# First feed-forward block of a hybrid decoder: four covered tiles in place of six, a longer run of zero products at the opening, and another order for the first halved unit of each block

## The chip, the core and the metric

One core of one Trainium2 chip runs the whole program. Its engines work side by side, each through its own queue in order: TensorE (PE; its weight loads are listed apart as PEld), VectorE (DVE), ScalarE (ACT), GpSimd (POOL) and SyncE (SP), which here only starts transfers. The metric is the device time of one execution in microseconds.

## What is computed

A decoder trunk of two layers on x, 512 tokens of width 1024, in float32. In a layer:

```
x = x + 1/2 * SwiGLU_a(RMSNorm(x))        # first FFN, width 2816
h = RMSNorm(x) @ W_mix_in                 # three token mixers share one projection
y = concat[shortconv | HGRN2 | FoX]
x = x + y @ W_mix_out
x = x + 1/2 * SwiGLU_b(RMSNorm(x))        # second FFN
swiglu(h, w_in, w_out) = (silu(gate) * up) @ w_out,   gate, up = split(h @ w_in)
rms_norm(x, gain) = x * rsqrt(mean(x*x) + 1e-6) * gain
```

The change touches the four FFNs (two of each layer), above all the first one, with which the program opens.

## The kernel before

**Number format.** Each float32 operand is cut into a high part, which ScalarE casts, and a low part, which VectorE gets as operand minus high part. A product is then three matmuls (`mm3`, L387): high by high, high by low, low by high.

**The two ways to compute an FFN.** D_FF is 22 tiles of 128 features, taken in pairs. The first `covered` tiles are *covered*: plain products over all 512 tokens, of x that has its gain but is not yet normalised (`cover`, L627). A pair of tiles takes four steps of two of the eight tiles of x; a step is 24 matmuls of 512 columns, and a pair 96. The results lie in four PSUM banks until 1/rms is known; "clear t" then multiplies the two banks of tile t by it, "silu t" and "values t" finish the tile. The purpose of the covered tiles is that TensorE has work while the norm is computed and the operands of the rest are built.

The rest is *halved* (`halved`, L781): a matrix product by two-by-two blocks with seven products instead of eight, P1 to P7, for a unit of two tiles. Each product is 24 matmuls of 256 columns, so a unit has 168. A product needs two things. Its *operand* on the x side is built once for each FFN: quarters of the normalised x ("x a b", `normalise` L746, four VectorE instructions), sums of them ("+ a b c d", L678), and then the two parts (`operand` L759: ScalarE L774 or L779, VectorE L775 or L779). P1 takes quarter 00, P5 00+01, P6 that plus 11, P4 that plus 10; P2 takes 10, P7 01+11, P3 11. Its *weights* are blocks 0 to 3 of w_in, or sums of them: P1 block 0, P2 block 1, P5 2+3, P6 the sum S of P5's block and block 0, P7 block 0 plus 2, P3 block 1 plus S, P4 block 3. Some sums are VectorE instructions ("sum", L829), some are transfers of GpSimd that add to what lies in the tile ("add" L816; "adds" L859, which adds S to block 1). `prepare` (L831) cuts the weights of a product in two parts (ScalarE L841, VectorE L843), three products ahead (`LEAD`), into one of three buffers `hl`; the buffer comes free when TensorE has finished the product three before.

**The order.** `ENTRY[covered]` is written by hand: at step n of the covered tiles (n = 4 to 2*covered-1), at the three first preparations, and after each product from then on, `deal(n)` (L663) issues the work listed under n. `follow` chains these instructions of ScalarE, VectorE, GpSimd and the transfers, so that each engine takes them just in the program's order. The first FFN has covered = 6 and its first 4 steps are the opening; the other three have covered = 4. `ORDER_IN` is the order of the seven products of a unit. `plan(covered)` (L80) works out a sequence of all products and when loads, sums and adds are issued; for the first unit it issues "adds" ahead of the first product, behind the preparation of P1, P2 and P6. After its product, P1 is copied out of its bank (g1, L933), P2 subtracted from it (L936) and given to silu; P6 is copied out (g2, L940) and P5 too (u2, L943); P7 then goes on summing in the bank that P6 was copied from.

The four banks of a unit's first three new sums are those of the first covered pair: P1 needs tile 0 cleared, and the third new sum needs tile 1 cleared.

**The opening.** `open_x` (L1715) and `idle` (L1743) start the program: two products of zeros (tile `none`) on TensorE, the gain, the first 128 columns of x transposed, one more product of zeros, and then the first matmuls (L445), high part of the weights first. Each product of zeros takes its bank anew.

Of the kernel before, what the change touches and what calls it, by code (L numbers as in the profile page):

```python
# [8 lines left out]
F32 = mybir.dt.float32  # L9
F32R = mybir.dt.float32r  # L10
# [15 lines left out]
P = 128  # L26
T = 512
# [8 lines left out]

ORDER_IN = ("P1", "P2", "P6", "P5", "P7", "P3", "P4")
ORDER_OUT = ("P2", "P1", "P5", "P6", "P7", "P3", "P4")
LEAD = 3
# [11 lines left out]
    },  # L51
# [5 lines left out]
    },  # L57
# [22 lines left out]
def plan(covered):  # L80
# [6 lines left out]
    into = lambda c: [  # L87
        ("I", f, p) for f in range(max(covered, c[0]), c[0] + c[1], 2) for p in ORDER_IN
    ]
# [25 lines left out]
    for u in dict.fromkeys((k, w) for k, w, _ in seq):  # L115
# [5 lines left out]
        if kind == "I":  # L121
            end = {0: "P7", 1: "P3", 2: "P5", 3: "P4"}
            m = split["P6"] - 1
            if w == covered:

                when(-1, 5, "add", u, 0, 2)
                when(-1, 6, "adds", u)
                continue
            else:
                begin[2] = m - 1 - AHEAD_SUM - AHEAD_LOAD  # L130
                begin[3] = split["P7"] - 2 - AHEAD_LOAD
                when(m - 1 - AHEAD_SUM, 5, "add", u, 2, 3)
                between(m - 1, m, "total", u, "S2")
                when(max(m, split["P2"]), 6, "adds", u)
                between(max(m, split["P1"]) + 1, split["P7"] - 1, "total", u, "S3")
        else:
            end = {0: "P7", 1: "P2", 2: "P3", 3: "P4"}
            begin[2] = split["P5"] - AHEAD_SUM - AHEAD_LOAD
            when(split["P5"] - AHEAD_SUM, 5, "add", u, 2, 3)
            if w[0]:  # L140
                when(split["P5"] + 1, 5, "add", u, 2, 0)
            else:
                between(split["P5"] + 1, split["P5"] + 2, "total", u, "S2")
            when(split["P5"] + 3, 5, "add", u, 0, 2)
            when(split["P6"] + 1, 5, "add", u, 2, 1)
# [38 lines left out]
class Trunk:  # L184
# [8 lines left out]
    def __init__(self, ctx, tc):  # L193
        self.tc = tc
        self.nc = tc.nc
        nc = self.nc
        self.const = ctx.enter_context(tc.tile_pool(name="const", bufs=1))
        self.res = ctx.enter_context(tc.tile_pool(name="res", bufs=1))
# [5 lines left out]
            tc.tile_pool(name="dram", bufs=1, space=bass.MemoryType.DRAM)  # L204
        )
        self.ident = self.const.tile([P, P], F32, tag="ident", name="ident")
        make_identity(nc, self.ident)
        self.ones_mean = self.const.tile([P, P], F32, tag="ones_mean", name="ones_mean")
        nc.vector.memset(self.ones_mean, 1.0 / D)
        self.epsc = self.const.tile([P, 1], F32, tag="epsc", name="epsc")  # L210
        nc.vector.memset(self.epsc, EPS)
        self.xT = self.res.tile([P, KD, T], F32, tag="xT", name="xT")

        self.none = self.res.tile([P, T], F32R, tag="inv", name="none")
        nc.vector.memset(self.none.bitcast(F32), 0.0)

        self.xh, self.xl = [None] * KD, [None] * KD
        self.uid = 0
        self.ntog = 0
        self.tab, self.tab_users = None, []  # L220
        self.chain = {}

# [184 lines left out]
    def stream_steps(  # L407
# [17 lines left out]
        while k < nk:  # L425
# [36 lines left out]
            for n, ((acc, cols, toks, *more), j) in enumerate(order):  # L462
                if pre is not None and n == len(order) // 2:
                    pre(k, True)
                if fine and n == len(order) // 2:
                    yield
# [160 lines left out]
    def cover(self, fp, w_in, w_out, covered, mean, begin):  # L627
# [35 lines left out]
        def deal(n):  # L663
            if n == mean and begin is None:
                squares()
            for what in filter(None, ENTRY[covered].get(n, "").split(", ")):
                name, *at = what.split()
# [25 lines left out]
        for f in range(0, covered, 2):  # L693
            banks = self.next4()

            def parts(k, kk, f=f):
# [8 lines left out]
                (lambda *a: self.open_x(x, gain, fp, *a)) if opening else None,  # L705
                None if opening else (lambda k, f=f: deal(2 * f + k // 2)), begin is None or f > 2,

# [73 lines left out]
    def halved(self, fp, w_in, w_out, covered, deal):  # L781
# [107 lines left out]
        u = seq[0][:2]  # L889
        for q in (2, 0, 3, 1):  # L890
            raw[u, q] = t = fp.tile(
                [P, 4, 2 * P], F32, tag=("mh", "ml")[q % 2], name=self.n("w"), bufs=2
            )
            S(nc.sync.dma_start(t, src(u, q)))
# [820 lines left out]
    def open_x(self, x, gain, fp, k, loaded=False):  # L1715
# [6 lines left out]
        if not loaded:  # L1722
            if k == 0:
                self.idle(2)
                self.begin_norm(gain, fp)
# [3 lines left out]
                self.load_open(0)  # L1729
                self.idle(1)  # L1730
                self.xb[1] = self.load_x(x, 1, fp, True)
# [11 lines left out]
    def idle(self, n):  # L1743

        for _ in range(n):
            b = self.bank("po")
            self.follow("p", self.nc.tensor.matmul(b, self.none[:, :P], self.none, start=True, stop=True))
# [27 lines left out]
def trunk_kernel(  # L1775
# [47 lines left out]
```

## Time and profile before

| | us |
|---|---|
| median of 3 runs | 1831.99 (1830.6 to 1832.21) |
| the profiled execution, its own time | 1832.37 |
| its span, first to last instruction | 1830.6 |
| TensorE busy (matmuls) | 1821.0 |
| VectorE busy | 1445.3 |
| ScalarE busy | 1001.7 |

The profile's times are microseconds from the start of the span. In a timeline a row has the start, the duration, engine, line of the kernel, operation and tiles, and in brackets the idle time before it with what ended it. A matmul's duration holds its pipeline, so for a run of matmuls it is the distance of their starts that counts. In the chain of waits the durations are already such distances.

### The profile page before, as it was taken

Reading aid. Unit: us, or ns where it says so; the run is one execution under the profiler, and the core shown is the slowest. Engines: PE = TensorE matmul, PEld = TensorE weight load, DVE = VectorE, ACT = ScalarE, POOL = GpSimd, SP = SyncE. Lnnn points to the kernel's source line nnn. Section 1 sums busy time; section 2 is a strip of 40 time slices with the busy share of each in tenths; the row PEclk is TensorE's granted clock in tenths of the full one; section 3 lists DMA queues with packets and bytes.
Section 4 is the critical chain, followed back from the end, with each engine's and each line's share of the span. In section 5 each row is a group of like instructions: output and inputs, shape, how many; then the busy total and the mean of one; then the engine's idle time right before and its main releaser. Section 6 shows DMA issues by size and latency. Waiting matters only on the chain.

```text
span 1830.6 us, 31999 instructions
## 1 busy us (share of the span) xinstructions
PE 1821.0 (99%) x12934; PEld 1674.7 (91%) x12934; DVE 1445.3 (79%) x1965; ACT 1001.7 (55%) x1414; POOL 185.1 (10%) x190
## 2 busy tenths in 40 slices
PE   9999999999999999999999999999999999999999
PEld 7899999888888899999889999998888888999997
DVE  8889786679677888879678887976777778888883
ACT  5455554465666465555445555555656655555552
POOL 0011120100000101112001111201000001020210
PEclk9999999999999999999999999999999999999999
DMA  7668783242543767868276787823425438677762
GB/s 214 177 134 189 177 180 94 68 124 68 127 110 96 216 136 168 193 165 174 81 202 140 174 183 190 163 69 84 114 74 127 119 98 217 161 152 196 154 135 92
DMA packets 249908, 262.38 MB, mean 143 GB/s; under 512 B 19816, under 2 KB 228464, under 8 KB 249760
## 3 DMA queue, kind: packets, MB, share of 16 engines
q1 hardware_dynamic: 193904, 192.15, 35.7%
q0 software_dynamic: 55840, 68.19, 23.4%
q8 instruction: 101, 1.65, 0.4%
q14 instruction: 47, 0.39, 0.1%
q10 hardware_dynamic: 16, 0.00, 0.0%
HBM read 226.15 MB, written 2.17 MB: 125 GB/s over the span
## 4 chain that ended last, share of the span: by engine, by line
PE 96%; ACT 1%; DVE 1%; DMA 1%; issue 0%; SPq 0%; DVEq 0%; ACTq 0%
PE mm L392 14%; PE mm L399 14%; PE mm L398 14%; PE sc L392 6%; PE sc L399 6%; PE sc L398 6%; PE pt L392 6%; PE pt L399 6%; PE pt L398 6%; PE po L392 4%; PE po L399 4%; PE po L398 4%; PE sc L1600 1%; PE po L1655 1%; PE sc L1414 1%; PE pt L1637 1%
## 5 line engine op out<-in xcount | busy, mean ns | idle before, releaser
L841 ACT CAST hl<-w 128x1024 fp32r<-128x1024 f32 x322 | 337.7, 1050 | 347.6 <-PE mm L399 81.9
L843 DVE TENSOR_TENSOR hl<-w,hl 128x1024 fp32r<-128x1024 f32 x322 | 392.5, 1220 | 87.2 <-ACT hl L841 87.0
L379 DVE TENSOR_TENSOR hl<-st,hl 128x1024 fp32r<-128x1024 f32 (+3 forms) x152 | 160.0, 1053 | 120.4 <-ACT hl L378 119.7
L378 ACT CAST hl<-st 128x1024 fp32r<-128x1024 f32 (+3 forms) x152 | 138.6, 912 | 176.3 <-PE po L399 81.5
L392 PE MATMUL mm<-xc,hl 128*128 128x256 f32 (+1 forms) x730 | 201.4, 276 | 0.3 <-ACT g L940 0.3
L399 PE MATMUL mm<-xc,hl 128*128 128x256 f32 x728 | 201.4, 277 | 0.0
L398 PE MATMUL mm<-xc,hl 128*128 128x256 f32 x728 | 201.2, 276 | 0.0
L392 PE MATMUL sc<-xc,hl 128*128 128x256 f32 (+1 forms) x530 | 146.4, 277 | 0.6 <-ACT g L940 0.6
L399 PE MATMUL sc<-xc,hl 128*128 128x256 f32 x528 | 146.1, 277 | 0.0
L398 PE MATMUL sc<-xc,hl 128*128 128x256 f32 x528 | 146.0, 277 | 0.0
L392 PEld LDWEIGHTS mm<-xc,hl 128*128 128x128 f32 x730 | 137.0, 188 | 0.8 <-ACT g L940 0.5
L398 PEld LDWEIGHTS mm<-xc,hl 128*128 128x128 f32 x728 | 136.8, 188 | 0.0
L399 PEld LDWEIGHTS mm<-xc,hl 128*128 128x128 f32 x728 | 136.6, 188 | 0.1
L392 PE MATMUL pt<-xc,hl 128*128 128x256 f32 (+1 forms) x482 | 132.7, 276 | 0.0
L398 PE MATMUL pt<-xc,hl 128*128 128x256 f32 x480 | 132.7, 276 | 0.0
L399 PE MATMUL pt<-xc,hl 128*128 128x256 f32 x480 | 132.6, 276 | 0.0
L392 PE MATMUL mm<-x,hl 128*128 128x512 f32 x272 | 108.8, 400 | 0.0
L399 PE MATMUL mm<-x,hl 128*128 128x512 f32 x272 | 106.1, 390 | 0.0
L398 PE MATMUL mm<-x,hl 128*128 128x512 f32 x272 | 105.9, 389 | 0.0
L392 PEld LDWEIGHTS sc<-xc,hl 128*128 128x128 f32 x530 | 99.5, 188 | 1.5 <-ACT g L940 1.0
L399 PEld LDWEIGHTS sc<-xc,hl 128*128 128x128 f32 x528 | 99.2, 188 | 0.1
L398 PEld LDWEIGHTS sc<-xc,hl 128*128 128x128 f32 x528 | 99.1, 188 | 0.0
(487 smaller groups left out, 5470.6 us busy)
## 6 DMA issues: line engine op xcount, KB each, us to landing
w<-in_ffn_w_in_dram SPq DMA_DIRECT2D x140, 512.0 KB
w<-in_ffn_w_out_dram SPq DMA_DIRECT2D x64, 512.0 KB
w<-in_ffn_w_out_dram POOLq DMA_DIRECT2D x56, 512.0 KB, 9.0
st<-in_w_mix_in_dram SPq DMA_DIRECT2D x80, 256.0 KB
w<-in_ffn_w_in_dram POOLq DMA_DIRECT2D x39, 512.0 KB, 8.1
st<-in_ffn_w_in_dram SPq DMA_DIRECT2D x70, 256.0 KB
w<-S POOLq DMA_DIRECT2D x35, 512.0 KB, 4.7
st<-in_ffn_w_out_dram SPq DMA_DIRECT2D x24, 512.0 KB
```

The source lines that it names most:

```text
L378: a = nc.scalar.copy(hi, src[:, c : c + w])
L379: b = nc.vector.tensor_sub(lo, src[:, c : c + w], hi)
L392: i = nc.tensor.matmul(acc[:, c], ah, bh[:, c], start=first and c.start == 0, stop=False, skip_group_check=True,)
L398: nc.tensor.matmul(acc, ah, bl, start=False, stop=False, skip_group_check=True)
L399: i = nc.tensor.matmul(acc, al, bh, start=False, stop=last, skip_group_check=True)
L841: A(nc.scalar.copy(hi, src))
L843: return lambda: V(nc.vector.tensor_sub(lo, src, hi))
L1414: nc.tensor.matmul(s2[:, :, t], e[:, i * P : (i + 1) * P], e2[:, :, t], start=True, stop=True)
L1600: mm = lambda *a, **k: E(nc.tensor.matmul(*a, skip_group_check=True, **k))
L1637: E(nc.tensor.transpose(tb[:, k * P : (k + 1) * P], to[u][:, j * P : (j + 1) * P], self.ident))
L1655: E(nc.tensor.matmul(self.ob[:, o], half[2][:, j, h].rearrange("p a d -> p (a d)"), part[:, at[0] : at[-1] + 1, :].rearrange("p b t -> p ( ...
```

## The change

The first FFN takes four covered tiles, and its `ENTRY` is a new one of its own, "opening". The other FFNs keep `ENTRY[4]`. All four take a new order for the seven products of their first unit, load its blocks in another order, and issue the first unit's "adds" behind the preparation of P2, which is now the fourth (so behind the first product, no longer ahead of it). The covered steps can be dealt work at their middle too (key 4.5). The tile of zeros is set first of all; four and three products of zeros are issued, for two and one, each group into one bank that is taken once.

```
 ORDER_IN = ("P1", "P2", "P6", "P5", "P7", "P3", "P4")
+ORDER_FIRST = ("P1", "P5", "P6", "P2", "P7", "P3", "P4")
...
-    6: {
-        7: "norm, x 0 0", 8: "x 1 0, clear 0, clear 1", 9: "silu 0, silu 1, x 0 1, P1, + 0 0 0 1",
-        10: "load, P2, values 0, values 1, x 1 1", 11: "P5, clear 2, + 0 0 1 1",
-        12: "silu 2, P6, clear 3, sum", 13: "values 2, silu 3, + 0 1 1 1, P3", 14: "P7, values 3, + 0 0 1 0",
-        15: "P4", 16: "clear 4", 17: "silu 4", 18: "values 4, clear 5", 19: "silu 5", 20: "values 5",
+    "opening": {
+        4.5: "load", 6: "norm", 7: "x 0 0, P1", 8: "x 0 1, + 0 0 0 1, P5", 9: "clear 0, x 1 1",
+        10: "sum, + 0 0 1 1, silu 0, P6", 11: "x 1 0, values 0, P2, clear 1, + 0 1 1 1", 12: "P7, silu 1",
+        13: "values 1, P3", 14: "+ 0 0 1 0, P4", 17: "clear 2", 18: "silu 2", 19: "values 2",
+        20: "clear 3", 21: "silu 3", 22: "values 3",
     },
...
-        ("I", f, p) for f in range(max(covered, c[0]), c[0] + c[1], 2) for p in ORDER_IN
+        ("I", f, p) for f in range(max(covered, c[0]), c[0] + c[1], 2)
+        for p in (ORDER_FIRST if f == covered else ORDER_IN)
...
                 when(-1, 5, "add", u, 0, 2)
-                when(-1, 6, "adds", u)
+                when(split["P2"], 6, "adds", u)
...
+        self.none = self.res.tile([P, T], F32R, tag="inv", name="none")
+        self.follow("v", nc.vector.memset(self.none.bitcast(F32), 0.0))
         self.ident = self.const.tile([P, P], F32, tag="ident", name="ident")
         make_identity(nc, self.ident)
...
-        nc.vector.memset(self.ones_mean, 1.0 / D)
+        self.follow("v", nc.vector.memset(self.ones_mean, 1.0 / D))
...
+                if deal is not None and n == len(order) // 2:
+                    deal(k, 0.5)
...
-            for what in filter(None, ENTRY[covered].get(n, "").split(", ")):
+            for what in filter(None, ENTRY[covered if begin is None else "opening"].get(n, "").split(", ")):
...
-                None if opening else (lambda k, f=f: deal(2 * f + k // 2)), begin is None or f > 2,
+                None if opening else (lambda k, half=0, f=f: deal(2 * f + k // 2 + half)), begin is None or f > 2,
...
-        for q in (2, 0, 3, 1):
+        for q in (2, 0, 1, 3):
...
-                self.idle(2)
+                self.idle(4)
                 self.begin_norm(gain, fp)
...
-                self.idle(1)
+                self.idle(3)
...
+        b = self.bank("po")
         for _ in range(n):
-            b = self.bank("po")
             self.follow("p", self.nc.tensor.matmul(b, self.none[:, :P], self.none, start=True, stop=True))
...
-            ffn1_w_in[l], ffn1_w_out[l], mix_norm[l], 4 if l else 6, 2,
+            ffn1_w_in[l], ffn1_w_out[l], mix_norm[l], 4, 2,
```

More of the change, by code (lines that the diff above doesn't have):

```diff
@@ L196, in __init__ @@
         nc = self.nc
+        self.uid = 0
+        self.ntog = 0
+        self.tab, self.tab_users = None, []
+        self.chain = {}
         self.const = ctx.enter_context(tc.tile_pool(name="const", bufs=1))
@@ L212, in __init__ @@
         self.xT = self.res.tile([P, KD, T], F32, tag="xT", name="xT")
-        self.none = self.res.tile([P, T], F32R, tag="inv", name="none")
-        nc.vector.memset(self.none.bitcast(F32), 0.0)
         self.xh, self.xl = [None] * KD, [None] * KD
[L218 to L221, printed above, removed]
     def build_consts(self, scratch):
```

## The prediction, as it was put on record

> **What bounds the kernel now.** I read the page's busy line first, then the chain of waits, then the timelines of single engines where an FFN begins.
>
> ```profile
> PE 1821.0 (99%) x12934; PEld 1674.7 (91%) x12934; DVE 1445.3 (79%) x1965; ACT 1001.7 (55%) x1414; POOL 185.1 (10%) x190
> PE 96%; ACT 1%; DVE 1%; DMA 1%; issue 0%; SPq 0%; DVEq 0%; ACTq 0%
> ```
>
> TensorE is the chain nearly everywhere. So the time falls only by fewer or faster matmuls, and any wait of TensorE that the change adds comes on top. What can be late is read at the FFNs' beginnings. First the prices of TensorE's work, from its timeline: a covered pair and the first halved unit of the second FFN, then the first halved unit of the opening.
>
> ```profile
> 616.00 0.39 PE L392 MATMUL mm<-x,hl 128*128 128x512 f32 x1
> 637.75 0.33 PE L392 MATMUL sc<-xc,hl 128*128 128x128 f32 x2
> 649.24 0.38 PE L392 MATMUL sc<-xc,hl 128*128 128x256 f32 x1 [0.31 <-ACT g L940]
> 657.77 0.33 PE L392 MATMUL pt<-xc,hl 128*128 128x128 f32 x2
> 78.90 0.33 PE L392 MATMUL mm<-xc,hl 128*128 128x128 f32 x2
> 98.07 0.33 PE L392 MATMUL po<-xc,hl 128*128 128x128 f32 x2
> ```
>
> A covered pair takes 637.75 - 616.00 = 21.75 us, a step a quarter of it, 5.44. A unit without waits takes 98.07 - 78.90 = 19.17, a product some 2.72. In the second FFN the first unit took 20.02: it waited at 649.24, where P7 begins, for the copy of P6's result (L940), and lost 0.85 in all. So where four tiles are covered, the entry is already at its limit.
>
> **The change part by part.**
>
> *Two tiles less covered:* 21.75 goes, 19.17 comes: -2.6 us. A further -0.2 comes from the norm, issued a step earlier, which frees a bank that the second pair's weight loads wait for (0 to -0.4, by this row of the waits):
>
> ```profile
> PEld po L392 <- DVE nt L539: 0.4, 1, 0.4
> ```
>
> *Zeros at the opening:*
>
> ```profile
> 1.62 1.65 PE L1747 MATMUL po<-none 128*128 128x512 f32 x2 [1.62 <-DVE none L215]
> 4.56 0.77 PE L1747 MATMUL po<-none 128*128 128x512 f32 x1
> 6.35 1.22 PE sc L445 x2
> 9.28 0.85 PE sc L445 x2
> 11.84 0.71 PE pt L445 x2
> 12.54 0.44 PE mm L1768 x4
> 13.41 0.23 PE sc L392
> ```
>
> The first two rows are TensorE's timeline, the rest the chain. Until 12 us two matmuls of 512 columns take 0.85; later one takes 0.23, and four transposes 0.44. The array ran at half rate until it had worked without a pause from 6.35 to about 12.1. (The column of the granted clock says 1.00 throughout and doesn't show this.) From 6.35 to 13.41 stand 12 such matmuls and 12 transposes; at the fast pitch they take 12 x 0.23 + 12 x 0.11 = 4.1 in place of 7.06. So the gain is at most 3.0; at least 0, if the zeros don't open the clock sooner. A loss has no room: the zeros start 0.25 earlier as the memset stands first, and four of them, 0.43 apart and without the pause for the bank, end at 3.1, before today's two (1.62 + 1.65); two more behind the one that ends at 5.33 end at 6.2, ahead of 6.35. I take 2.3, nearer to the upper end, since zeros then stand on both sides of the first transposes and nearly close the gap before 6.35. The covered steps that follow are bound by TensorE, so it stays won. The Trainium skill (TensorE: Matmul & The Clock Gate, Part 1) has the array at half rate until one window of some 3.4 us was busy, with windows that run free of the kernel's start; the ratio 0.85 to 2 x 0.23 agrees. By it the clock would open between 4.8 and 8.2, an estimate, and the gain be 3.0 to 2.
>
> *The first FFN's entry.* Here the cover that goes has a price. It hid VectorE:
>
> ```profile
> 616.00:637.70 21.70, 21.70 (x97) 18.00 (x96) 21.67 (x30) 9.79 (x10) 3.45 (x3) 1.00 0.81 236
> 34.17 1.02 PE L551 MATMUL po<-sqa,ones_mean 128*128 128x512 f32 x2
> 34.21 1.04 ACT L378 CAST hl<-st 128x1024 fp32r<-128x1024 f32 x1 [2.18 <-DMA st<-in_ffn_w_in_dram]
> 36.53 0.68 ACT L300 ACTIVATE nr<-po,epsc 128x512 f32<-128x512 f32 x1
> 38.57 0.69 DVE L539 SCALAR_TENSOR_TENSOR nt<-po,nt 128x512 f32<-128x512 f32 x1 [0.69 <-ACT nt L300]
> 39.76 0.69 DVE L543 TENSOR_TENSOR inv<-nr,nt 128x512 f32<-128x512 f32 x1
> 614.81 1.67 DVE L752 SCALAR_TENSOR_TENSOR xn<-xT,gain,inv 128x256 f32<-128x256 f32 x4
> 616.40 1.22 DVE L379 TENSOR_TENSOR hl<-st,hl 128x1024 fp32r<-128x1024 f32 x1
> 653.00 1.22 DVE L775 SCALAR_TENSOR_TENSOR xc<-xn,xc 128x1024 fp32r<-128x1024 f32 x1
> ```
>
> The first row is a window, the second FFN's last covered pair; its third busy figure is VectorE's, 21.67 of 21.70. What TensorE waits for in this queue starts when 1/rms is there (614.81, the first quarter of x) and ends with the low part of P4's operand (653.00 to 654.2), the last that the norm yields: 39.4 us there. In the opening the norm comes late: the squares' sum at 34.17 can't be earlier, as it needs all of x, and the cast at 34.21 is ahead of it on ScalarE. With the norm moved one step ahead, its first instruction follows at 35.3 instead of 36.53, and 1/rms, which came at 39.76 + 0.69 = 40.45, is there at 39.2 (all in before's time; the zeros shift both sides). TensorE, one covered pair later, begins P1 at 78.90 - 21.75 - 0.2 = 56.95 and would begin P4 six products later, at 73.4. That leaves 34.2 us from 1/rms. VectorE's queue up to P4's low part, by the new entry and the program's order, goes by these rows:
>
> ```profile
> 631.50 0.68 DVE L643 TENSOR_TENSOR gi<-sc,inv 128x512 f32<-128x512 f32 x1
> 632.10 0.68 DVE L644 TENSOR_TENSOR ui<-sc,inv 128x512 f32<-128x512 f32 x1
> 632.70 1.21 DVE L678 TENSOR_TENSOR xn<-xn,xn 128x1024 f32<-128x1024 f32 x1
> 633.83 1.22 DVE L843 TENSOR_TENSOR hl<-w,hl 128x1024 fp32r<-128x1024 f32 x1
> 634.97 1.22 DVE L678 TENSOR_TENSOR xn<-xn,xn 128x1024 f32<-128x1024 f32 x1
> 643.08 0.42 DVE L734 TENSOR_TENSOR hq<-gi,ui 128x256 f32<-128x256 f32 x1
> 643.41 0.42 DVE L731 SCALAR_TENSOR_TENSOR hq<-gi,ui 128x256 f32<-128x256 f32 x1
> 647.78 1.23 DVE L779 TENSOR_TENSOR xc<-xn,xc 128x1024 fp32r<-128x1024 f32 x1 [1.02 <-ACT xc L779]
> ```
>
> Back to back, instructions of 1024 elements start 1.14 apart, those of 512 0.60, those of 256 0.34; a quarter of x takes 1.6 (614.81 to 616.40). In the queue stand the low parts of 2 covered steps, 7 weights and 7 operands, 4 sums of quarters and S: 21 x 1.14 = 23.9. Four quarters make 6.4, four clears 2.4, four "values" 1.3, the subtraction of P2 0.6. Together 34.6. To this come stretches in which the next in order needs ScalarE's high part of what VectorE has just made, as at 647.78: once each for P1's, P5's, P6's and P4's operand 1.1, and 1.0 in smaller ones, 5.4. So 39.2 + 34.6 + 5.4 = 79.2, and with the handovers 79.9, against 73.4 + 0.1: 6.4 us of waits. Walked through by ends: P1's operand 44.6, P5's 50.9, P6's 60.6, P6's weights 61.7, P2's 62.8, x 1 0 64.4, "values" 65.1, P2's operand 66.8, the first bank of "clear 1" 67.4, the sum for P7 69.1, P7's operand 71.4, P3's weights 72.9, P4's weights 76.5, P4's sum 77.6, its operand 79.9. So P1, P5 and P6 start in time; P2, due at 65.2, waits for its bank to 67.4; P7 waits to 72.2 for P6's copy, which stands on ScalarE behind P7's operand and P3's weights; P4 waits from 77.6 to 79.8. Bounds: at the least the queue without its 5.4, +1; at the most 1.7 later, if the cast's transfer, which ended a wait of 2.18, doesn't come earlier with the rest, +8. I take the walk, +6.5, as its whole length, 40.7, is near the 39.4 measured.
>
> *The other three FFNs.* Their ENTRY stays; the order of the first unit and "adds" change. In P2's old place P5 is prepared, whose block must have landed for S (626.51) already; no wait. P2, though, is now prepared as the fourth, where P5 stood, and "adds" goes behind it:
>
> ```profile
> 626.51 1.22 DVE L829 TENSOR_TENSOR S<-w,w 128x1024 f32<-128x1024 f32 x1
> 635.34 0.88 POOL L859 DMA_DIRECT2D w<-S  x1 [2.18 <-DVE hl L843]
> 641.94 1.23 DVE L843 TENSOR_TENSOR hl<-w,hl 128x1024 fp32r<-128x1024 f32 x1 [1.62 <-ACT hl L841]
> 647.66 1.04 ACT L841 CAST hl<-w 128x1024 fp32r<-128x1024 f32 x1
> 648.60 0.58 ACT L940 ACTIVATE g<-sc 128x512 f32<-128x512 f32 x1
> DMA to landing us min/median/max: 4.5/4.7/7.2
> 646.00:650.00 4.00, 3.69 (x32) 3.50 (x32) 2.98 (x3) 4.00 (x6) 0.00 (x0) 1.00 0.33 109
> ```
>
> Today GpSimd starts "adds" at 635.34, 0.3 behind P2's low part (633.83 + 1.22). After the change that low part is the one at 641.94, so "adds" starts at 643.5 and lands 4.7 later, 648.2 (the sixth row: all such transfers). Its sum is P3's weights, and their cast (647.66 now) waits on ScalarE for it. Behind this cast stand P6's copy (L940) and so P7: 648.2 + 0.95 + 0.58 + handover = 649.8 for 649.24. The transfers are busy until about 647 (the last row), so I take 5.0 to landing: P7 0.9 later than now. The subtraction for P2 and its silu, which stood ahead, now come between P3's weights and P4's operand, whose low part then is 0.5 late. About +1.2 for each FFN, +3.6 for three; by the landings' ends +0.8 x 3 = 2.4 and +3.5 x 3 = 10.5. The moved loads, the middle step for "load" and the reordered memsets cost nothing: SP and GpSimd issue them with time to spare, hidden by the covered pairs, and the blocks are there at 626.51. In the first FFN "adds" (62.8 + 0.3 + 4.7 = 67.8) lands before P3's cast gets its turn there, at 70.6.
>
> Sum: -2.6 - 0.2 - 2.3 + 6.5 + 3.6 = +5.0. On the profiled execution's 1832.37 (span 1830.6) that is 1837.4; on the median of the runs, 1831.99, it is **1837.0**.
>
> **The rivals.**
>
> 1. *No new wait (faster).* The mechanism: VectorE's queue keeps up in the opening because its waits for ScalarE vanish between other work and the norm ends earlier; it decides at P4, if the low part is there by 73.4 instead of 79.8. With the new order then also freeing P6's copy in the others (the 0.85 lost there goes three times): -2.6 - 0.2 - 2.3 - 2.5 = -7.6, 1824.4. For it: P2's subtraction and silu leave the place ahead of P6's copy. Against it: VectorE's 21.67 of 21.70, and 39.4 us for the same queue in the second FFN.
> 2. *The cheap ends meet:* clock open at once (-3.0), "adds" landing in 4.5 (+2.4), the opening's waits at 6: +2.6, 1834.6, within the measurement.
> 3. *The clock doesn't open earlier* (the change doesn't do what it says): +7.3, 1839.3.
> 4. *Contention:* "adds" lands in 7.2 everywhere (+10.5): +11.9, and with the late cast +13.6, 1845.6.
>
> **How the numbers follow.** Forecast 0.50 (its own range 1835.7 to 1841), rival 1 0.17, rival 2 0.22, rival 3 0.06, rival 4 0.05. A measurement of this kernel can tell 0.2%, 3.7 us, from no change. Faster: rival 1, 0.17. Same: rival 2, 0.22. Slower: the rest, 0.61. The range from 1828 to 1842 leaves out rival 4 and most of rival 1.
>
> **What would show it.** Covered: the first FFN's P1 starts near 54.6 us (56.95 less 2.3). Zeros: pairs of L445 at 0.46 instead of 0.85, and the first L392 near 11 instead of 13.4. VectorE: no idle time but for ScalarE from 1/rms to P4's low part, and TensorE waiting there for a cleared bank, for L940 and for P4's operand. Others: L859 starts some 8 us later against P1, ScalarE's L841 waits for its landing, and P7 begins over 11.9 us behind P1 (11.5 now). Wrong I would be above all if VectorE finished P4's operand within 34 us of 1/rms, or if the first units of the other FFNs took less than 20.0 us.

## The result and the profile after

The changed kernel takes 1842.77 us in the median of six runs (1840.87 to 1850.93), the kernel before 1831.3 on the same chip (1830.17 to 1832.81): 11.5 us or 0.7% slower, ratio 1.007 with a 95% interval of 1.0051 to 1.0088. The forecast was +5.0, its range ended at 1842. The sign was right, the size less than half.

The profiled execution, the shortest of the six, took 1840.87 us (span 1839.1), 8.5 more than that of before, which at 1832.37 lies near the longest of that kernel's runs. Its lines are shifted: L395, L401, L402 are L392, L398, L399 of before, L846 and L848 are L841 and L843, L864 is L859, L945 is L940. The opening, from the chain of waits:

```profile
8.31 0.47 PE sc L448 x2
11.04 0.23 PE sc L395
```

Pairs that took 0.85 take 0.47, and the first covered matmul starts at 11.04 instead of 13.41: the zeros do what they were put there for.

The first FFN's entry, in TensorE's timeline at P1, P2, P7, P4 and the next P1, then VectorE's end of 1/rms and its rows ahead of P4:

```profile
54.41 0.34 PE L395 MATMUL sc<-xc,hl 128*128 128x128 f32 x2
64.81 0.35 PE L395 MATMUL pt<-xc,hl 128*128 128x256 f32 x1 [1.95 <-DVE gi L648]
69.55 0.39 PE L395 MATMUL sc<-xc,hl 128*128 128x256 f32 x1 [1.67 <-ACT g L945]
78.03 0.55 PE L395 MATMUL sc<-xc,hl 128*128 128x256 f32 x1 [2.56 <-ACT hl L846]
82.29 0.33 PE L395 MATMUL pt<-xc,hl 128*128 128x128 f32 x2
```

```profile
36.06 0.69 DVE L548 TENSOR_TENSOR inv<-nr,nt 128x512 f32<-128x512 f32 x1
76.06 1.23 DVE L780 SCALAR_TENSOR_TENSOR xc<-xn,xc 128x1024 fp32r<-128x1024 f32 x1 [1.12 <-ACT xc L779]
77.20 0.68 DVE L951 TENSOR_TENSOR u<-u,sc 128x512 f32<-128x512 f32 x1
```

P1 starts where it was forecast (54.6), and P2, P7 and P4 wait as forecast: for a cleared bank, for P6's copy, and behind P4's operand. (At P4 the profile names a cast, L846, for the next unit; that cast and L951, VectorE's reading of the bank that P4 goes on summing in, both end at 77.9, so this profile doesn't tell them apart. In e11 below it names the reading.) By the distance of starts (2.22, 1.95 and 2.84, less 0.11 each) the waits are 6.7 us. But from P4's start to the next P1 there are 4.26 us where a product takes 2.72. Windows of 3.4 us, laid so that one begins where the clock falls, show why; the third figure from the end is the granted clock, the first busy figure TensorE's, with the number of its instructions in brackets:

```profile
67.40:70.80 3.40, 1.73 (x15) 1.52 (x14) 3.12 (x5) 3.40 (x6) 0.00 (x0) 1.00 0.02 5
74.20:77.60 3.40, 1.27 (x11) 1.06 (x10) 2.28 (x3) 2.63 (x3) 0.00 (x0) 1.00 0.00 0
77.60:81.00 3.40, 2.97 (x14) 3.00 (x15) 3.40 (x5) 0.52 (x2) 0.00 (x0) 0.52 0.00 0
81.00:84.40 3.40, 3.40 (x31) 3.40 (x31) 2.94 (x4) 1.46 (x2) 2.19 (x2) 0.98 0.30 55
```

Behind the wait for P4 the array runs at half rate for 3.4 us: 14 matmuls, from P4's start on, where the next window, at full rate, has 31. The product takes 4.26 - 2.72 = 1.5 us longer, which no step of the prediction has.

In a later FFN (the second; first three rows of TensorE's timeline, where P1, P7 and P4 begin, then GpSimd, ScalarE and VectorE):

```profile
639.31 0.33 PE L395 MATMUL sc<-xc,hl 128*128 128x128 f32 x2
651.82 0.39 PE L395 MATMUL sc<-xc,hl 128*128 128x256 f32 x1 [1.32 <-ACT g L945]
658.54 0.36 PE L395 MATMUL sc<-xc,hl 128*128 128x256 f32 x1 [1.01 <-DVE u L951]
```

```profile
645.01 0.88 POOL L864 DMA_DIRECT2D w<-S  x1 [8.51 <-DVE hl L848]
```

```profile
650.22 1.04 ACT L846 CAST hl<-w 128x1024 fp32r<-128x1024 f32 x1 [2.09 <-DMA w<-S]
651.17 0.59 ACT L945 ACTIVATE g<-sc 128x512 f32<-128x512 f32 x1
```

```profile
656.57 1.22 DVE L780 SCALAR_TENSOR_TENSOR xc<-xn,xc 128x1024 fp32r<-128x1024 f32 x1 [0.51 <-ACT xc L779]
657.72 0.68 DVE L951 TENSOR_TENSOR u<-u,sc 128x512 f32<-128x512 f32 x1
```

"Adds" starts behind P2's low part, lands 5.1 later, the cast of P3's weights waits for it, P6's copy stands behind that cast, and P7 begins 12.5 us behind P1 (11.5 before). That is the forecast chain. P4 then waits too, by 1.0, for VectorE to read P7's bank (L951), a row that stands behind P4's operand. The list of waits (us in total, times, the longest) has these places, and two in the second layer's mix. That for the transfer (L1605) before doesn't have; one of 0.5 for L1142 it has too, but in the first layer's mix (390.6), which is 0.6 us shorter now:

```profile
PE sc L395 <- ACT g L945: 4.2, 3, 1.7
PE sc L395 <- DVE u L951: 2.0, 2, 1.0
PE sc L1605 <- DMA A<-b: 1.0, 1, 1.0
PE mm L395 <- DVE zf L1142: 0.5, 1, 0.5
```

From P1 to the first product with w_out, the way back, the later FFNs take 52.10, 51.67 and 51.96 us (50.07, 50.16 and 50.06 before): +5.4.

### The profile page after: what moved, and what is told of

Its sections match the earlier page's. It is cut to its first block, busy times and chain, and to the rows that moved or that the text cites. A ratio compares the mean times of both kernels' runs of the same rounds, so it can differ in the third digit from the quotient of the medians.

```text
span 1839.1 us, 32169 instructions
## 1 busy us (share of the span) xinstructions
PE 1818.1 (99%) x13010; PEld 1675.8 (91%) x13010; DVE 1450.9 (79%) x1967; ACT 1005.8 (55%) x1420; POOL 187.2 (10%) x192
## 4 chain that ended last, share of the span: by engine, by line
PE 83%; issue 6%; DVE 5%; DMA 2%; ACT 2%; POOL 0%; SPq 0%; DVEq 0%; ACTq 0%; POOLq 0%
PE mm L395 11%; PE mm L402 11%; PE mm L401 11%; PE sc L395 6%; PE sc L401 6%; PE sc L402 6%; PE pt L395 6%; PE pt L401 6%; PE pt L402 6%; PE po L395 3%; PE po L402 3%; PE po L401 3%; PE sc L1605 1%; DVE hl L382 1%; PE po L1660 1%
## 5 line engine op out<-in xcount | busy, mean ns | idle before, releaser
L846 ACT CAST hl<-w 128x1024 fp32r<-128x1024 f32 x328 | 343.7, 1049 | 347.1 <-PE pt L402 82.0
L848 DVE TENSOR_TENSOR hl<-w,hl 128x1024 fp32r<-128x1024 f32 x328 | 400.0, 1221 | 89.2 <-ACT hl L846 89.1
L395 PE MATMUL sc<-xc,hl 128*128 128x256 f32 (+1 forms) x819 | 226.9, 278 | 8.8 <-ACT g L945 4.2
L402 PE MATMUL sc<-xc,hl 128*128 128x256 f32 x816 | 226.3, 277 | 0.0
L401 PE MATMUL sc<-xc,hl 128*128 128x256 f32 x816 | 226.2, 277 | 0.0
L395 PE MATMUL pt<-xc,hl 128*128 128x256 f32 (+1 forms) x699 | 192.5, 276 | 1.9 <-DVE gi L648 1.9
L401 PE MATMUL pt<-xc,hl 128*128 128x256 f32 x696 | 192.4, 276 | 0.0
L402 PE MATMUL pt<-xc,hl 128*128 128x256 f32 x696 | 192.2, 276 | 0.0
L395 PEld LDWEIGHTS sc<-xc,hl 128*128 128x128 f32 x819 | 154.4, 189 | 10.1 <-ACT g L945 4.8
L402 PEld LDWEIGHTS sc<-xc,hl 128*128 128x128 f32 x816 | 153.9, 189 | 0.1
L401 PEld LDWEIGHTS sc<-xc,hl 128*128 128x128 f32 x816 | 154.0, 189 | 0.0
L402 PE MATMUL mm<-m,hl 128*128 128x256 f32 x504 | 139.6, 277 | 0.0
L401 PE MATMUL mm<-m,hl 128*128 128x256 f32 x504 | 139.3, 276 | 0.0
L395 PE MATMUL mm<-m,hl 128*128 128x256 f32 x504 | 139.3, 276 | 0.0
L395 PEld LDWEIGHTS pt<-xc,hl 128*128 128x128 f32 x699 | 131.0, 188 | 2.1 <-ACT u L948 2.1
L401 PEld LDWEIGHTS pt<-xc,hl 128*128 128x128 f32 x696 | 130.7, 188 | 0.0
L402 PEld LDWEIGHTS pt<-xc,hl 128*128 128x128 f32 x696 | 130.6, 188 | 0.0
L395 PE MATMUL mm<-xc,hl 128*128 128x256 f32 (+1 forms) x393 | 108.5, 276 | 1.8 <-DVE u L951 1.0
L395 PE MATMUL mm<-x,hl 128*128 128x512 f32 x272 | 108.8, 400 | 0.0
L402 PE MATMUL mm<-xc,hl 128*128 128x256 f32 x392 | 108.4, 276 | 0.0
```

The costliest lines, as they stand in the source:

```text
L395: i = nc.tensor.matmul(acc[:, c], ah, bh[:, c], start=first and c.start == 0, stop=False, skip_group_check=True,)
L401: nc.tensor.matmul(acc, ah, bl, start=False, stop=False, skip_group_check=True)
L402: i = nc.tensor.matmul(acc, al, bh, start=False, stop=last, skip_group_check=True)
L846: A(nc.scalar.copy(hi, src))
L848: return lambda: V(nc.vector.tensor_sub(lo, src, hi))
```

## The experiments

My theory after the profile: VectorE bounds the first FFN's entry (as forecast); the clock falls behind those waits, in each run by its own phase; the late accumulation bounds the later entries. The rivals stand with each run. Times are medians beside the kernel before on the same chip.

**e1, the zeros alone.** Edit: the kernel before, with the memset of `none` first and

```
-                self.idle(2)
+                self.idle(4)
-                self.idle(1)
+                self.idle(3)
```

> The kernel before with the zeros' part alone: memset first, four and three zero matmuls on one bank. My theory: the whole gain of the zeros is won at the opening and kept, since what follows is bound by TensorE: the pairs of L445 0.46 us apart instead of 0.85, the first covered matmul at 11.0 instead of 13.4, -2.4 us, so about 1829 beside 1831.3. Rival: part of the 11 us lost by the whole change comes from here (the zeros put the steps out of phase with the loads, or make the runs scatter): then no gain, or a loss, and a spread of the runs as wide as the changed kernel's 10 us.

Measured: 1828.74 beside 1830.72, ratio 0.9992 (0.9983 to 1.0001): -2.0, and runs within 3.2 us. The theory's size holds for the median, though the interval just reaches no change. In this one profile the clock opened only at 10.1 (first covered matmul at 12.37):

```profile
10.11 0.47 PE pt L445 x2
12.37 0.23 PE sc L392
```

The next experiment, with the old zeros, has it at 10.8 and the kernel before at about 12.1. So where the clock opens differs from run to run, with the same zeros by 3 us and more. Of the twelve profiles with the new zeros, ten have the first covered matmul at 10.3 to 11.2 in TensorE's timeline (10.80 in the changed kernel's first) and two at 12.1 (this one and e7's); the two with the old zeros have it at 12.4 (e2) and 13.2 (before). Their means are 1.9 apart, near the 2.0. The forecast's estimate for the opening of the clock, 4.8 to 8.2, held in the changed kernel, where the chain has a pair of 0.46 at 7.41, and not here.

**e2, the new order in the later FFNs alone.** Edit to the kernel before:

```
+        for p in (ORDER_FIRST if f == covered == 4 else ORDER_IN)
-                when(-1, 6, "adds", u)
+                when(split["P2"] if covered == 4 else -1, 6, "adds", u)
-        for q in (2, 0, 3, 1):
+        for q in ((2, 0, 1, 3) if covered == 4 else (2, 0, 3, 1)):
```

> The kernel before with the new order of products, the new order of the first loads, and the late accumulation of the sum into block 1, all in the three later FFNs alone; the first FFN keeps its six covered tiles and the zeros are as before. My theory: the copy of P6's result waits on ScalarE behind the cast of P3's weights, which waits for the accumulating transfer that now starts behind P2's low part, and P4 then waits for VectorE to read P7's bank behind P4's operand: P7 about 0.9 later and P4 about 1.0 later in each, read from the changed kernel as +2.0, +1.5 and +1.9, together +5.4: 1836.7 beside 1831.3. The granted clock stays at 1.00 behind these waits of at most 1.3 us, and the runs agree within 3 us. Rival: the order in the later FFNs costs only the 3.6 that I forecast, or nothing, and what is missing lies in the opening: 1831 to 1835.

Measured: 1837.11 beside 1830.72, +6.4, ratio 1.004 (1.0027 to 1.0052); the three first units took 51.90, 52.17 and 52.52, together +6.3. The theory holds, a little more than read; the forecast of 3.6 was too small. In one run of five, the longest (1840.69), the mean clock was 0.998, so that there it didn't stay at 1.00 as expected; that run has no profile. The waits of TensorE name both parts, here for two of the three FFNs (us, times, longest; the third sums in other banks, 1.4 and 1.0):

```profile
PE sc L394 <- ACT g L942: 2.9, 2, 1.7
PE sc L394 <- DVE u L948: 1.8, 2, 1.0
```

**e3, the wait for P4 filled with work.** Edit to the changed kernel, ahead of the call of `product` (the matmuls read an operand that is there already, and their result is not used):

```
+            if n == 6 and begin is not None:
+                h = self.xc["P1"][0].rearrange("p k c -> p (k c)")
+                for _ in range(10):
+                    self.follow("p", nc.tensor.matmul(work[u, "c"], h[:, :P], h[:, :T], start=True, stop=True, ...))
```

> The changed kernel with ten more matmuls of 512 columns, their result thrown away, between P3 and P4 of the first FFN's first unit, where TensorE waits 2.5 us for P4's operand: the wait is filled with work and P4 starts as late as before. My theory: the wait leaves TensorE idle long enough that its granted clock falls to 0.50 from 77.5 to 81 us, which costs 1.7 us in the profiled execution and more in others; filled, the clock stays at 1.00 there, the start of P4 stays near 78.0, the unit ends 1.7 earlier, the median falls by 2 to 4 us (1839 to 1841 beside 1842.8), and the spread of the runs, 10 us, falls to about 3. Rival: the fall of the clock has to do with the phase of the chip or its load and not with this wait: it stays in the profile, and the median stays at 1842.8 or rises by the additional work.

Measured: 1838.03 beside 1830.72, +7.3 where the whole change costs +11.5, all runs within 3 us. P4 starts at 78.11, as late as without the fill, and the clock stays at 1.00 (third row). Not all of the difference is the clock's: in this profile the second mix is 1.8 shorter than in the changed kernel's. And the clock fell at another wait, that for P2's bank:

```profile
61.80:65.20 3.40, 1.45 (x13) 1.29 (x12) 2.95 (x5) 2.49 (x3) 0.00 (x0) 0.97 1.21 205
65.20:68.60 3.40, 3.40 (x18) 3.40 (x18) 3.35 (x4) 2.04 (x3) 0.00 (x0) 0.53 0.48 94
75.40:78.80 3.40, 2.92 (x16) 2.23 (x15) 2.66 (x3) 2.59 (x3) 0.00 (x0) 1.00 0.00 0
```

There it cost almost nothing, since P7's wait, next in line, shrank from 1.95 to 0.43. So a half-rate stretch ahead of another wait is taken out of that wait, and the one behind the last wait is paid in full. The pair, with the same start of P4, work in place of the wait, and no fall, speaks for the idle time as what makes the clock fall: without the fill the third row's window would hold 0.7 us of work, from 78.11 on. As the windows lie differently in each run, one profile of each doesn't show it alone; e11 tests it from the other side.

**e4, a second copy of block 1 to accumulate into.** Edit to the changed kernel:

```
-                when(split["P2"], 6, "adds", u)
+                when(-1, 6, "adds", u)
-            G(nc.gpsimd.dma_start(raw[u, 1], sums[u], accum_op=ALU.add))
+            G(nc.gpsimd.dma_start(raw.get((u, 4), raw[u, 1]), sums[u], accum_op=ALU.add))
+        raw[u, 4] = t = fp.tile([P, 4, 2 * P], F32, tag="xl6", name=self.n("w"))
+        S(nc.sync.dma_start(t, src(u, 1)))
```

P3's weights are then made from this copy.

> The changed kernel, with block 1 loaded a second time into a tile of its own in each FFN's first unit, so that the accumulation of the sum for P3's weights goes into that copy and needn't wait until P2's weights are made; it is issued at the start of the unit's work, as in the kernel before. My theory: the cast of P3's weights no longer waits for the landing, P6's copy and P7 come 0.9 earlier in each later FFN, and P4's operand, which stands behind these casts, about as much: -1.2 to -1.8 for each of three, so 1837.4 to 1839.2 beside 1842.8. Rival: transfers, not their late start, are what is short in these stretches; the additional 0.5 MB then makes the landing later, and nothing is won: 1842.8 or above.

Measured: 1836.72 beside 1830.72, +6.0: 5.5 of the 11.5 are gone. The later first units take 50.20, 50.18 and 50.12; P7 waits for no more than 0.2 us, and P4's wait is down to about 0.6.

So the late start of "adds" is the cause in the later FFNs; the 0.5 MB more does no harm. In this profile the clock fell twice in the opening, each time behind a window with little work:

```profile
62.90:66.30 3.40, 1.50 (x13) 1.33 (x12) 2.99 (x4) 1.81 (x3) 0.00 (x0) 0.98 1.11 195
66.30:69.70 3.40, 3.40 (x18) 3.35 (x16) 3.12 (x4) 2.75 (x4) 0.00 (x0) 0.52 0.35 55
76.50:79.90 3.40, 1.41 (x12) 1.44 (x12) 3.38 (x4) 1.87 (x2) 0.00 (x0) 0.99 0.00 0
79.90:83.30 3.40, 3.40 (x19) 3.40 (x18) 3.40 (x5) 0.96 (x2) 0.66 (x2) 0.51 0.00 0
```

**e5 and e12, the changed kernel again, unedited.**

> The changed kernel once more, unedited, for a second profile of its opening beside the others on the same chip. My theory, from three profiles so far: the granted clock goes by stretches of about 3.4 us whose phase against the kernel differs from run to run; a stretch in which TensorE is busy for 1.5 us or less (1.27, 1.41, 1.45 and 1.50 so far) is followed by one at 0.50, and one with 1.73 or more is not. The waits of P2, P7 and P4 in the first FFN's first unit are the same 2.2, 1.9 and 2.8 us, so the fall may come at another place, or twice, or not at all. The median again about 1842 beside 1830.7, the spread wide. Rival: the fall belongs to P4's wait as such: it comes again near 77.5 us and nowhere else.

Measured: 1844.01 beside 1829.46 (1839.97 to 1852.17): +14.6, where the first six runs gave +11.5, so a difference of two experiments' medians is uncertain by some 3 us for this kernel. The three waits are the same (2.22, 1.96, 3.03), and the clock fell behind P4's wait again, for two windows. The profiled execution was one of the long ones, 1852.17, and shows something else. Here are 20 us of the way back, first of the first profile and then of this one; TensorE is busy throughout at a clock of 1.00:

```profile
120.00:140.00 20.00, 20.00 (x179) 20.00 (x179) 15.44 (x17) 9.63 (x12) 3.53 (x3) 1.00 0.62 122
```

```profile
77.00:80.40 3.40, 2.64 (x12) 2.67 (x13) 3.40 (x6) 0.64 (x1) 0.00 (x0) 0.51 0.00 0
80.40:83.80 3.40, 3.40 (x18) 3.40 (x17) 2.36 (x4) 1.12 (x2) 1.89 (x2) 0.50 0.20 37
...
120.00:140.00 20.00, 20.00 (x172) 20.00 (x172) 15.23 (x16) 8.90 (x10) 3.53 (x3) 1.00 0.53 114
```

172 matmuls instead of 179: their pitch, the distance from start to start, is 0.1178 us instead of 0.1133, from 84 us to the end of the first FFN at 321, and back to 0.1133 afterwards. From the sum of squares to that of the next stage 330.3 us pass instead of 320.2; some 1.7 of that goes to the second half-rate window, and most of the rest to this pitch.

> The changed kernel unedited, for a third profile of its opening. My theory: waits of 2.1, 1.8 and 2.7 us again; a stretch of 3.4 us with 1.5 us of TensorE's work or less is followed by one at 0.50; a time near 1842 if the pitch of the halved products stays at 0.113 us, near 1851 if they run at 0.118 from the opening on. Rival: the long time of the second profile had another cause, and the pitch there was chance: then a time near 1851 would go with 0.113.

Measured: 1841.38, clock down once, behind P7's wait; from P3's last matmul to P4 there were 1.42 us instead of 2.84 for it, so this window cost next to nothing. The window ahead of the fall had 1.56 us of work:

```profile
66.60:70.00 3.40, 1.56 (x13) 1.36 (x13) 3.03 (x3) 3.40 (x5) 0.00 (x0) 1.00 0.03 6
70.00:73.40 3.40, 3.40 (x18) 3.40 (x17) 3.40 (x6) 2.03 (x3) 0.00 (x0) 0.50 0.02 5
```

Behind the entry the pitch was 0.113, though P4's own matmuls (78.2 to 81.0) went at 0.118. All thirteen runs of the changed kernel, by the mean clock that each lists: 1839.97 at 1.000; 1840.87, 1841.38 and 1842.75 at 0.999; 1842.4 to 1844.95 in six and 1850.93 to 1852.17 in three, all at 0.998. One half-rate window of 3.4 us takes 0.0009 off that mean, so these are runs with none, one and two. The means of the first three groups are 1.7 us apart, and the one run without any is still 10.5 above the kernel before. Of the kernel before, the seventeen runs beside e5 list 1.000 each.

**e6, the first FFN alone.** Edit to the changed kernel: `ORDER_FIRST`, the load order and the late "adds" only where `begin is not None`.

> The changed kernel with its new order of products, new order of loads and late accumulation in the first FFN alone; the three later FFNs are as in the kernel before. My theory: the later first units go back to 50.1 us from P1 to the first O product, -5.4 to -6.3 against the changed kernel: 1836.5 to 1837.4 beside 1842.8, and what is left of the loss, 6 to 7 us beside the kernel before, is the opening's. Rival: the later FFNs cost the 3.6 that I forecast: 1839.2, and the opening holds 8 to 9.

Measured: 1835.34 beside 1829.46, +5.9; the later first units are back at 50.17, 50.16 and 50.07. As the whole change cost 11.5 at first, the later FFNs hold 5.6, which agrees with their units; beside the 14.6 of e5, on this chip, it would be 8.7, of which the units explain 5.4. The theory holds for the units. With -2.0 for the zeros the rest of what this kernel keeps of the change costs +7.9. Its windows bound the clock's rule from the other side; 1.66 us of work was enough, 1.49 was not:

```profile
62.70:66.10 3.40, 1.66 (x14) 1.69 (x15) 3.40 (x5) 1.38 (x2) 0.00 (x0) 1.00 1.16 214
66.10:69.50 3.40, 1.49 (x13) 1.29 (x12) 2.97 (x3) 3.34 (x5) 0.00 (x0) 1.00 0.09 17
69.50:72.90 3.40, 3.40 (x18) 3.40 (x19) 3.40 (x6) 2.08 (x3) 0.00 (x0) 0.53 0.02 5
```

**e7, the low parts of the first FFN's operands left out.** The high part stands in for them, so this kernel's result is not the full product. Edit to the changed kernel, in `operand`:

```
-        self.follow("a", a), self.follow("v", v)
+        self.follow("a", a)
+        if self.light:
+            lo = hi
+        else:
+            self.follow("v", v)
```

> The changed kernel; in the first FFN the low parts of the seven operands are left out (the high part stands in for them, so TensorE and ScalarE do as much as before, and VectorE has seven instructions of 1024 elements less, 8 us). My theory: VectorE's queue is what TensorE waits for there; P2, P7 and P4 start without their waits of 2.1, 1.8 and 2.7 us, and with these goes the fall of the clock (1.7 in the profile, more in the median): -8.3 to -10, 1832.5 to 1834.5 beside 1842.8. Rival: ScalarE's casts or the transfers of the first unit's weights hold these products just as long: more than half of the waits stays, and the time stays above 1838.

Measured: 1840.63 beside 1829.46, 3.4 less than the changed kernel's median on this chip and not 8 to 10. P2's wait shrank to 0.3 and P4's went, as VectorE's queue explains. P7's grew to 3.3, and ScalarE's timeline says why:

```profile
69.70 1.04 ACT L853 CAST hl<-w 128x1024 fp32r<-128x1024 f32 x1 [1.52 <-DMA w<-S]
70.65 0.59 ACT L952 ACTIVATE g<-sc 128x512 f32<-128x512 f32 x1
```

There too, the cast of P3's weights waits for the accumulating transfer, which landed at 69.7, and P6's copy is behind it. In the unedited opening this limit is hidden behind VectorE's. The theory fell as to the size: VectorE is the first limit, not the only one.

**e8, a better version.** Edit: e1, and in `ENTRY[4]`

```
-        12: "silu 1, P3", 13: "+ 0 0 1 0, values 1", 14: "P4", 17: ...
+        12: "P3", 13: "+ 0 0 1 0, silu 1", 14: "P4, values 1", 17: ...
```

> The kernel before with the zeros' part, six covered tiles and the old order, and in the later FFNs' list of duties the silu of tile 1 one step later, behind P3's operand, and the values of tile 1 one step later. My theory: -2.0 from the zeros as measured alone; P6's copy no longer stands behind the silu of tile 1 and the casts, so P7's wait of 0.5 to 0.85 goes in each of three: -1.4 to -2.5, together 1826.2 to 1827.3 beside 1830.7. Rival: the silu now delays P4's operand as much as P7 wins: 1828.7, as with the zeros alone.

Measured: 1827.51 beside 1829.46, ratio 0.9988 (0.9979 to 0.9997): 2 us faster than the kernel before, with six covered tiles and the old order. The later first units take 49.64, 49.74 and 49.65, 0.4 less each, and P7 begins without a wait. The gain is less than the 0.5 to 0.85 expected; beside e1 it is within the measurement.

**e9, e7 and e4 together.**

> The changed kernel with two things at once: the low parts of the operands left out in the first FFN (the high part stands in for them), and block 1 loaded twice so that the accumulation needn't wait for P2's weights. In the run without the low parts alone, P2 and P4 started without a wait, but P7 waited 3.5 us for P6's copy, which stood on ScalarE behind the cast of P3's weights, which waited for the accumulating transfer (issued at 62.2, landed at 69.7). My theory: VectorE's queue is the first limit of that entry and the landing of the accumulation the second, with nothing third behind them; with both gone the first unit takes 19.2 to 20 us from P1 on, the clock stays at 1.00, and the later units take 50.2: 1829.5 - 2.0 (zeros) - 2.8 (pair for unit) + 0.5 = 1825 beside 1829.5, up to 1827 with the 2 us that the second mix lost in most kernels with four covered tiles. Rival: four covered tiles cost something else, in the rest of the program: 1830 or above though the first unit is free of waits.

Measured: 1831.76 beside 1830.0, ratio 1.0011 (1.0003 to 1.0019). Eleven of twelve runs list a clock of 1.000, and all but one lie within 2.3 us. P7 still waits 1.8:

```profile
66.57 0.61 ACT L303 ACTIVATE gi<-gi 128x512 f32<-128x512 f32 x1
67.09 1.03 ACT L853 CAST hl<-w 128x1024 fp32r<-128x1024 f32 x1
68.02 0.59 ACT L954 ACTIVATE g<-sc 128x512 f32<-128x512 f32 x1
```

ScalarE's order is a third limit: the silu of tile 1 and a cast stand ahead of P6's copy. My "nothing third" fell. With the computation lightened and no fall of the clock, four covered tiles still don't win. By the pieces, 1.8 of waits and 1.4 more in the second mix beside -2.9 for the pair and -2.0 for the zeros, this kernel should have been some 1.7 ahead of the kernel before and was 1.8 behind; what makes up the difference wasn't found.

**e10, P4's operand one step later.** Edit to the changed kernel: `14: "P4"` becomes `15: "P4"` in both lists.

> The changed kernel with P4's operand made one step later in every FFN, so that on VectorE the reading of P7's bank, into which P4 accumulates, stands ahead of the operand's low part and not behind it. My theory: P4's wait in the later FFNs, 1.2 us, is the 0.68 us reading queued behind the low part; it falls by about 0.6 in each of three, -1.8; in the opening it changes little, as the queue is full there: 1841 beside 1843. Rival: the high part of the operand, now behind the cast of the next unit's weights on ScalarE, holds P4 as long or longer: no change or up to +2.

Measured: 1860.03 beside 1830.0 (1849.93 to 1861.13), 17 above the changed kernel: the theory fell, and the rival's 2 is far too small. VectorE reads P7's bank early now, but two instructions for the next products come ahead of the operand's low part:

```profile
655.85 0.68 DVE L951 TENSOR_TENSOR u<-u,sc 128x512 f32<-128x512 f32 x1
656.45 1.22 DVE L848 TENSOR_TENSOR hl<-w,hl 128x1024 fp32r<-128x1024 f32 x1
657.58 1.22 DVE L834 TENSOR_TENSOR S<-w,w 128x1024 f32<-128x1024 f32 x1
658.72 1.22 DVE L780 SCALAR_TENSOR_TENSOR xc<-xn,xc 128x1024 fp32r<-128x1024 f32 x1
```

P4's second matmul waits 2.0 to 2.2 in every FFN, and its runs list mean clocks of 0.995 to 0.997, three to five half-rate windows. The profiled run is the shortest of seven; what the others have above it wasn't seen.

**e11, a longer wait for P4.** Edit to the changed kernel: three more copies of the low part's instruction in `operand` for P4 in the first FFN.

> The changed kernel with the low part of P4's operand computed four times over in the first FFN (the same result, 3.4 us more of VectorE), so that P4 waits about 6 us instead of 2.7. My theory: a wait of 6 us leaves at least one whole stretch of 3.4 us with TensorE busy for less than 1.5 us, whatever the phase, so the clock falls to 0.50 behind it in every run: 3.4 later by the wait and 1.7 or more by the clock beside an execution of the changed kernel in which nothing fell, so 1844.5 to 1848; and if the pitch of 0.118 us between matmuls, seen for 230 us in one profile of the changed kernel in place of 0.113, is what a return of the clock in the middle of a product can leave behind, more of the runs than a quarter are 7 to 10 us above the others. Rival: the fall has nothing to do with the length of the wait: +3.4, about 1846 in the median, but with the clock at 1.00 behind P4's wait; or the pitch is independent of it: no run, or as few as before, above 1850.

Measured: 1847.78 (four runs from 1846.6 to 1847.9, one at 1855.83); every run lists 0.997 or 0.998. P4 waited 6.33, for the reading of P7's bank by the profile (L958 here, L951 of the changed kernel), and the clock was at 0.50 behind it:

```profile
79.30:82.70 3.40, 0.06 (x1) 0.09 (x1) 3.33 (x5) 0.00 (x0) 0.00 (x0) 0.68 0.00 0
82.70:86.10 3.40, 3.40 (x16) 3.40 (x17) 3.40 (x4) 0.63 (x1) 0.00 (x0) 0.50 0.00 0
...
120.00:140.00 20.00, 20.00 (x172) 20.00 (x171) 15.25 (x17) 9.02 (x11) 3.52 (x3) 1.00 0.44 125
```

The clock's part of the theory holds. The profiled run, the long one, again has the pitch of 172 matmuls in 20 us, up to the end of the first FFN. It wasn't more frequent, one run of five, so that a return of the clock brings it about isn't shown.

## Why the prediction was wrong in size

| step | forecast | measured | from |
|---|---|---|---|
| pair for a unit, bank | -2.8 | -2.9 | P1 24.5 earlier, 2.4 of it by the zeros; a unit is 19.17 |
| zeros | -2.3 | -2.0 | e1, whose interval just reaches 0 |
| waits of the opening | +6.5 | +6.7 | starts of P2, P7, P4 |
| clock behind the last wait | none | +1.5 | P4's product in the first profile; e3, e11 |
| later FFNs | +3.6 | +5.4 | first units; e2, e4, e6 |
| second layer's mix | none | +1.8 | from the sum of squares ahead of it to the next, 260.46, before 258.68 |

The sum is +10.5; the medians gave +11.5 and, in e5, +14.6. The half-rate window is paid twice in e5's profile and hardly in e12's. In the profiled pair itself, where the zeros gave -2.4, the sum is +10.1 and the spans are 8.5 apart: before's profile has two stretches with the slower pitch (280 to 310 and 1760 to 1790 us, about 1.2 us each) where the changed kernel's has none; the changed kernel's has another, at 870 to 890 us, and a first mix that is 0.6 shorter.

No single step holds the 6.5 us that the forecast missed: the later FFNs have 1.8 of them, the second mix 1.8, a half-rate window that is paid 1.5, the zeros 0.3. The rest is less than the medians of this kernel differ by.

- *Covered tiles, zeros, VectorE's walk: right.* 1/rms was forecast at 39.2 less 2.3 and ended at 36.75; P2, P7 and P4, forecast at 67.4, 72.2 and 79.8 less 2.3, started at 64.81, 69.55 and 78.03. Only P4 was late against the walk, by 0.5: its operand was complete at 77.29, but the reading of P7's bank (L951), which stands behind the operand on VectorE and ends at 77.88, wasn't in the walk.
- *The step that failed first*, in the order of the program, is "6.4 us of waits" as the whole price of the entry. It took the matmuls behind a wait to run as fast as before it, and so put the clock's price at nothing; the first profile has 1.5 there. The clock column that the prediction itself read was at 1.00 in all of before, where TensorE never idles for more than 0.5 us at a time from 6.35 us on. The Trainium skill (TensorE: Matmul & The Clock Gate, Part 1) was used for the opening and not for the waits that the change makes. By its section "Why this matters for your kernels", gaps of more than about 3 us bring the half rate back; here gaps of 2.1 to 2.8 us did, so going by it would have found no fall either. The same page has the windows run free of the kernel's start; the fall at P2, P7 or P4 by turns agrees.
- *The term that was mis-sized* is "about +1.2 for each FFN". P7 was 0.5 to 1.0 later, as forecast (0.9), but P4 then lost another 1.0 in each, where the forecast had some 0.3 for an operand 0.5 late: the profile names L951 for it, which no term has. The transfer's landing, 5.1, 4.6 and 5.0 in the three, was rightly priced (5.0).
- *The rivals.* "No new wait" fell with the three waits of the opening, "the cheap ends meet" with waits of 6.7 and a landing that wasn't 4.5, and "the clock doesn't open earlier" with pairs of 0.47. "Contention" gave 1845.6, nearer in number than the forecast, but its mechanism isn't there: "adds" landed in 4.9 in the median, not in 7.2.
- *Open.* The second mix was 1.4 to 2.7 us longer in nine of ten profiles with four tiles covered first (not in e3's), and in none of the four with six. In the first profile 1.5 of it are the waits at L1605, for a transfer, and at L1142. Why they are there wasn't found. What starts and ends the pitch of 0.118 us is open too; in the first profile it is there from P2's start behind its wait, at 64.8, to the wait for P4, and the kernel before, which has no such waits, has it for short stretches (280 to 310 us).

## What to carry to other kernels

Cover that is taken away must be priced at the engine that it hid: add up that engine's queue from the moment that its input is there to the last thing TensorE needs, and this sum was right to 0.5 us here. Then price the last of the waits that come out twice: once as idle time, and once more for what TensorE does afterwards, if a stretch of 3.4 us would be left with less than half its work (1.56 us or less here). An accumulating transfer belongs where its source is ready, if need be into a copy of its own, because whatever waits for its landing holds the whole queue of the engine that waits.

## What the runs showed of the hardware

- A window of about 3.4 us in which TensorE was busy for 1.56 us or less (seven windows above) was followed by one at a granted clock of 0.50; windows with 1.66 or 1.73 were not. Behind a half-rate window with 2.97 us of work or more the clock came back; behind one with 2.64 (e5) a second such window followed. Where a window begins differs from run to run, so the same waits make it fall at P2, P7 or P4, or, by the mean clock of one run (1.000), not at all.
- The granted-clock column shows that fall, but said 1.00 at the start of the program while pairs took 0.85 us instead of 0.47.
- Matmuls of 256 columns have two pitches, 0.1133 and 0.1178 us, at the same granted clock. Both long profiles kept the slower from the first FFN's entry to its end, 8 us in all.
